# Inverse square roots of a hybrid decoder block: one power on GpSimd in place of a seed and three Newton steps on VectorE

## The chip, the cores and the metric

The kernel runs on one core of a Trainium2 chip. That core has five engines, each with its own instruction queue that runs in order: TensorE (PE in the profile, with its weight loads as PEld), VectorE (DVE), ScalarE (ACT), GpSimd (POOL) and SyncE (SP), which here issues nearly all DMAs. The metric is the device time of one execution in microseconds (us).

## The reference

A decoder layer on 2048 tokens of 1024 channels, float32, with 16 learned meta tokens ahead. What is computed:

```
n1    = rmsnorm(h, norm1_g);  proj = n1 @ w_in              # 1024 x 1024
u, v  = halves of proj
ys    = state space on u (32 groups of 16 channels, 64 complex states), GELU, gate
yp    = trailing means over 2, 4, 8, 16 tokens of v, minus v, times a matrix per group
mixed = concat(rmsnorm(ys, ssm_norm_g), rmsnorm(yp, pool_norm_g));  h = h + mixed @ w_out
n2    = rmsnorm(h, norm2_g)
h     = h + (silu(n2 @ w_gate) * (n2 @ w_up)) @ w_down      # 2816 wide
out   = rmsnorm(h, final_norm_g) without the meta tokens
rmsnorm(x, g) = x * rsqrt(mean(x * x) + 1e-6) * g
```

There are five such norms. Each needs, for every token, one inverse square root of a mean of squares.

## The kernel before

**Tiling.** The tokens form 16 slices of 128 rows (two halves b = 0, 1 of eight slices t each); a seventeenth slice holds the 16 meta tokens. Every float32 product is done as three products of split operands: an operand is cut into a rounded part and a remainder (`split`), ScalarE writing the rounded part and VectorE the remainder, and `mm3` (L123 to L125) multiplies three of the four pairs.

**Stages.** First the input projection of slices 1, 2, meta, 3 to 8, while VectorE and GpSimd work out the tables of the state space (`params`, then eight `units`). Then the state space of b = 0 (`ssm_unit`) together with the projection of slices 9 to 16. Then the output projection: for each of 16 slices `out_mm` multiplies the pooled half and the state-space half of the mixed tokens by `w_out`; in its first eight turns `ssm_unit` of b = 1 runs along. Then the feed-forward network, whose products are formed as seven products of half-size blocks instead of eight (gate and up in `seven`, the down projection in `dmm` and `take`).

**Where inverse square roots are taken.** `rsqrt_into` is called 51 times:

- `stats`, 17 times, one column: the norm of a slice of input tokens. Its result `rs` scales the projected slice when ScalarE moves it out of PSUM (`put_u` L221, `put_v` L228).
- `out_mm`, 16 times, two columns: the norms of both halves of the mixed tokens. TensorE sums the squares into PSUM (`pss`, L814), VectorE scales them into `rv`, and the result `rsp` is used by four operations `hx` on VectorE that add the products to the residual and so free PSUM banks.
- once at the end of each half b, eight columns: the norm ahead of the feed-forward network (`rs2`).
- `finish`, 16 times, one column: the final norm, used by the two operations that scale the output row.

Before the change one call is the scaling `rv` (one operation, two in `out_mm`), then eleven VectorE operations on a tile of 128 x 1, 2 or 8 numbers: a shift (`rsh`, L91), the seed (L93), and three times a square (`rt`, L87), a product (`rt`, L96) and an update (L96). `tt` (L87), `ts` (L91, L93) and `stt` (L96) are helpers, so many operations of the kernel share these lines and are told apart by their tiles.

**What sets the order.** The program is written in the order above, but a planner reorders it when it is built: it places every instruction on its engine's queue by dependencies, priorities and its own estimate of times. Small operations of one call thus stand between larger ones of other calls. At run time each queue is strictly in order, and an instruction waits for semaphores of other engines. The tiles `rv`, `rsh` and `rt` come from a pool with four buffers.

Of the kernel before, what the change touches and what calls it, by code (L numbers as in the profile page):

```python
# [9 lines left out]
F32 = mybir.dt.float32  # L10
# [14 lines left out]
T = 8  # L25
# [14 lines left out]
def kernel(  # L40
# [57 lines left out]
    def rsqrt_into(y, ss, shape, terms):  # L98
        """y = 1 / sqrt(ss * scale + eps); terms: (slice, scale, eps)."""
        n = ss.shape[0]  # L100
        v = small.tile([P] + shape, F32, name="rv", tag="rv")[:n]
        sh = small.tile([P] + shape, I32, name="rsh", tag="rsh")[:n]
        t = small.tile([P] + shape, F32, name="rt", tag="rt")[:n]
        for sl, scale, eps in terms:
            ts(v[sl], ss[sl], scale, M_, eps, A_)
        ts(sh, v.bitcast(I32), 1, ALU.logical_shift_right)
        ts(y.bitcast(I32), sh, -1, M_, 0x5F3759DF, A_)
        for _ in range(3):
            tt(t, y, y, M_)
            stt(t, t, -0.5, v, M_, M_)  # L110
            stt(y, t, 1.5, y, A_, M_)

    def split(hi, lo, src, scale=None, e=V):
        """hi + lo = src (* scale per partition)."""
        if scale is None:
            A.copy(hi, src)  # L116
            tt(lo, src, hi.bitcast(F32), S_, e)
        else:
            A.activation(hi, src, AF.Copy, scale=scale)
            stt(lo, src, scale, hi.bitcast(F32), M_, S_)  # L120
# [5 lines left out]

# [1 line left out]
    ident = const.tile([P, P], F32, name="ident")  # L128
    make_identity(nc, ident)
    ones = const.tile([P, 1], F32, name="ones")  # L130
    V.memset(ones, 1.0)
    ss2 = const.tile([P, 2, NB * T], F32, name="ss2")
    rs2 = const.tile([P, NB * T], F32, name="rs2")
# [22 lines left out]
    def yview(b):  # L156
        """Outputs of the state space, [c, 128 channels, t, channel]."""
        return xu[b].rearrange("c g t h -> c (g t h)").rearrange("c (k t e) -> c k t e", k=4, t=T)

# [1 line left out]
    slices = [(meta, 2 * T)] + [(xv[b][:, t, :], P) for b in range(NB) for t in range(T)]  # L161
# [36 lines left out]
    def load_w(w, cols, spare=(), order=range(KD), then=lambda: None):  # L198
        """Two resident parts of a [D, D] weight, rows scaled."""
        hs, ls = [None] * KD, [None] * KD  # L200
        for n, k in enumerate(order):
            if n < len(spare):
                raw = spare[n]
            else:
                raw = raw_p.tile([P, D], F32, name="wraw", tag="hx")
            SY.dma_start(raw, w[k * P:(k + 1) * P, :])
            if n == 0:
                then()
            hi = wb_p.tile([P, D], F32R, name=f"wh{k}", tag=f"wh{k}")
            lo = wb_p.tile([P, D], F32R, name=f"wl{k}", tag=f"wl{k}")  # L210
            split(hi, lo, raw, cols(k))
            hs[k], ls[k] = hi, lo
        return hs, ls
# [90 lines left out]

# [1 line left out]
    par = ExitStack()  # L306
# [20 lines left out]
    def params():  # L327
# [43 lines left out]
        def exp_into(y, xx):  # L371
            """y = exp(xx), xx is overwritten."""
            k = pa_([P, G], "ek")
            ki = pa_([P, G], "eki", I32)
            ts(xx, xx, -87.0, ALU.max, 88.0, ALU.min)
            ts(k, xx, 1.4426950408889634, M_, MAGIC, A_)
            ts(k, k, -MAGIC, A_)
            stt(xx, k, -0.693359375, xx, M_, A_)
            stt(xx, k, 2.12194440054690583e-4, xx, M_, A_)
            cs = [1.0 / math.factorial(i) for i in range(1, 9)]  # L380
            ts(y, xx, cs[7], M_)
            for c in (cs[6], cs[5], cs[4], cs[3], cs[2], cs[1], cs[0]):
                stt(y, y, c, xx, A_, M_)
            ts(y, y, 1.0, A_)
            ts(k, k, 8388608.0, M_, 127.0 * 8388608.0, A_)
            V.tensor_copy(ki, k)
            tt(y, y, ki.bitcast(F32), M_)
# [121 lines left out]
    def grow(ct, st, w1, w2, n, ck, sk, e1, e2):  # L509
        """Table entries n .. 2n - 1 from 0 .. n - 1 and entry n."""  # L510
        lo, hi = slice(0, n), slice(n, 2 * n)
# [71 lines left out]

    # first two slices side by side: the weights arrive as they are used
    banks = [mm_tile(f"pj{q}") for q in range(4)]
# [59 lines left out]

# [1 line left out]
    ssm = ExitStack()  # L647
    ss_p = ssm.enter_context(tc.tile_pool(name="ssm", bufs=1))

    def rotate(o, tmp, vv, cc, sg, sign, eng=V):  # L650
        """o = vv * (cos + sign * i sin), halves real and imaginary."""
        tt(o, vv, cc, M_)
# [98 lines left out]

# [1 line left out]
    wo = ExitStack()  # L753
# [8 lines left out]
    def out_pool(b, t):  # L762
        """The pooled half of a slice of mixed tokens, by channel."""
        pin = wo_p.tile([P, 4, NCH], F32, name="pin", tag="pin")
# [11 lines left out]
    def out_ssm(b, t, mh, ml, sq):  # L776
        """The half of the state space, and the squares of both."""
        pt = tr_tile("pg")
# [76 lines left out]

# [1 line left out]
    gu = ExitStack()  # L857
# [12 lines left out]
    def turn(b, t):  # L870
        """A normalised row block, by channel, in place."""
        r = norm_row(b, t)
# [16 lines left out]
    def combos(b11, b12, b21, b22, put):  # L889
        """The seven right operands of a two by two product, in place."""  # L890
        put("b11", b11)
# [11 lines left out]
    def x_rows(b, t, direct=()):  # L903
        """The operands of the slice pair (t, t + 4): some are used at once."""
        ra, rb = turn(b, t), turn(b, t + HALF)
# [9 lines left out]
    def w_rows(m):  # L915
        """The sums of the weights of the down projection, rows of tiles 2 m and 2 m + 1."""
        ra, rb = [xa_p.tile([P, D], F32, name="wr", tag="raw", bufs=4) for _ in range(2)]
# [6 lines left out]
    def x_stage(b, i, n):  # L924
        """Operands i .. i + n - 1 from their rows."""
        for nm in XN[i:i + n]:
# [35 lines left out]
    def wset(w, f0):  # L962
        """Parts of a pair of weight tiles for the seven products."""
        r0, r1 = load_raw(w, f0), load_raw(w, f0 + 1)
# [8 lines left out]
    def seven(ws, c, done, early=False):  # L973
        """c(i, j) = weight tile i of the pair times token half j, one product a step."""
        a11, a12, s2, s3, s1, a22, s4 = ws
# [36 lines left out]
    def gate_up(b, f0, wg=None, wu=None):  # L1012
        """Without wu the products with the gate's weights come first, with it they alternate."""
        gt = wc_p.tile([P, 2, 2, 512], F32, name="gt", tag="gt", bufs=3)
# [41 lines left out]

# [1 line left out]
    NM = NF // 2  # L1058
# [90 lines left out]
    def take(i, n, o):  # L1149
        """Adds product i of slice pair n to the blocks that it belongs to."""  # L1150
        b, t = pairs[n]
# [114 lines left out]
```

## Time and profile before

| | |
|---|---|
| time, median of 3 runs | 1911.99 us (1908.38 to 1915.63) |
| profiled execution, span from first to last instruction | 1911.4 us; the page gives no other time of it, and the median of the runs is 0.6 us longer |
| PE busy | 1831.1 us (96%) |
| DVE busy | 1355.2 us (71%), 2553 instructions |
| ACT busy | 677.4 us (35%) |
| POOL busy | 781.4 us (41%), 568 instructions |
| DMA | 298.41 MB, mean 156 GB/s |

How to read it. A stage is a stretch of the span, counted in us from its first instruction. A row of a view by stages gives the stretch, its length, and for each engine its busy time and the number of instructions in it, then the granted TensorE clock (1.00 is full), the share of time the DMA engines were busy and their rate. A row of waits reads "who waited, at which line <- engine, tile and line it waited for: us in total, times, longest". A row of a timeline gives start, duration, engine, line, operation, output <- inputs and shapes; a bracket at its end is the idle time before it and what ended it. Matmuls overlap: 128 x 512 matmuls start 0.23 us apart and last 0.39 us each, so a busy share near 100% can hide small gaps.

### The profile page before, as it was taken

What the parts mean: (1) busy time and instruction counts of PE and PEld (TensorE: products, weight loads), DVE (VectorE), ACT (ScalarE), POOL (GpSimd) and SP (SyncE); (2) the same over time, 40 slices, a digit from 0 to 9 for tenths busy, and PEclk for the clock granted to TensorE, in tenths of its full rate; (3) what the DMA queues carried; (4) which work ended last, traced back from release to release, by engine and by line L of the source; (5) the groups of instructions that cost most, each with busy time, mean ns of one, the idle gap of its engine ahead of it and who ended that gap; (6) DMA issues with size and microseconds to landing.
All of it is one profiled execution on the core that took longest, in us unless ns stands there. A gap on an engine that the chain in (4) does not pass through costs nothing.

```text
span 1911.4 us, 24270 instructions
## 1 busy us (share of the span) xinstructions
PE 1831.1 (96%) x8497; PEld 1502.8 (79%) x8497; DVE 1355.2 (71%) x2553; ACT 677.4 (35%) x1228; POOL 781.4 (41%) x568
## 2 busy tenths in 40 slices
PE   7998996899998999999999999999999999999998
PEld 6776785778887788888887788888888888888876
DVE  6996988998687866666668876666676344445876
ACT  4232334333355332333325333333323343333331
POOL 1583314632143564554546876666562000003300
PEclk9998998899999999999999999999999999999999
DMA  5254425433354443444435663455447765536762
GB/s 179 80 162 159 138 95 171 151 131 121 128 179 152 143 154 94 154 150 137 155 96 183 206 214 127 149 171 176 138 140 234 210 201 178 152 105 209 243 190 90
DMA packets 260524, 298.41 MB, mean 156 GB/s; under 512 B 17149, under 2 KB 204049, under 8 KB 255537
## 3 DMA queue, kind: packets, MB, share of 16 engines
q1 hardware_dynamic: 260304, 296.84, 48.6%
q8 instruction: 67, 1.10, 0.2%
q14 instruction: 57, 0.46, 0.1%
q0 software_dynamic: 96, 0.01, 0.0%
HBM read 202.37 MB, written 96.53 MB: 156 GB/s over the span
## 4 chain that ended last, share of the span: by engine, by line
PE 54%; DVE 18%; issue 15%; DMA 7%; ACT 2%; POOL 2%; SPq 0%; DVEq 0%; POOLq 0%; ACTq 0%
PE pr L125 13%; PE pr L124 13%; PE pr L123 13%; PE pd L124 2%; PE pd L123 2%; PE pd L125 2%; DMA hd<-h_d 2%; DVE z L693 1%; DMA c<-c_d 1%; DVE st L87 1%; DVE wcl L87 1%; PE po L123 1%; PE po L124 1%; PE po L125 1%; DVE rt L87 1%
## 5 line engine op out<-in xcount | busy, mean ns | idle before, releaser
L87 DVE TENSOR_TENSOR wcl<-raw,wch 128x512 fp32r<-128x512 f32 x176 | 178.0, 1014 | 37.6 <-ACT wch L116 36.8
L87 DVE TENSOR_TENSOR fl<-fr,fh 128x512 fp32r<-128x512 f32 x168 | 116.1, 700 | 121.6 <-ACT fh L116 121.5
L116 ACT CAST wch<-raw 128x512 fp32r<-128x512 f32 x176 | 108.5, 620 | 263.2 <-PE pr L124 238.2
L116 ACT CAST fh<-fr 128x512 fp32r<-128x512 f32 x168 | 95.5, 583 | 190.5 <-PE pd L124 165.4
L116 ACT CAST wch<-s 128x512 fp32r<-128x512 f32 x132 | 81.9, 621 | 224.0 <-PE pr L124 177.1
L87 POOL TENSOR_TENSOR s<-raw 128x512 f32<-128x512 f32 x44 | 68.8, 1563 | 183.3 <-DVE wcl L87 85.3
L87 DVE TENSOR_TENSOR wcl<-s,wch 128x512 fp32r<-128x512 f32 x132 | 117.2, 888 | 19.9 <-ACT wch L116 19.8
L87 POOL TENSOR_TENSOR db22h<-db22h,hd 128x512 f32<-128x512 f32 x4 | 5.2, 1295 | 257.0 <-DVE db22h L87 257.0
L123 PE MATMUL po<-wh,mh 128*128 128x512 f32 x256 | 103.5, 404 | 3.1 <-DVE hx L96 2.4
L123 PE MATMUL pj<-wh,xh 128*128 128x512 f32 x256 | 100.6, 402 | 2.5 <-ACT xh L116 2.3
L124 PE MATMUL pj<-wl,xh 128*128 128x512 f32 x256 | 102.9, 403 | 0.0
L125 PE MATMUL pj<-wh,xl 128*128 128x512 f32 x256 | 101.8, 402 | 0.0
L124 PE MATMUL po<-wl,mh 128*128 128x512 f32 x256 | 100.7, 393 | 0.0
L125 PE MATMUL po<-wh,ml 128*128 128x512 f32 x256 | 100.4, 393 | 0.0
L87 POOL TENSOR_TENSOR wr<-wr 128x512 f32<-128x512 f32 x44 | 67.3, 1529 | 70.2 <-DMA wr<-in_w_down_dram 65.9
L87 POOL TENSOR_TENSOR tmp<-z,pk 64x512 f32<-64x512 f32 x32 | 50.8, 1588 | 110.1 <-issue 109.2
L87 DVE TENSOR_TENSOR gt<-gt,ut 128x512 f32<-128x512 f32 x88 | 93.9, 1068 | 0.0
L87 DVE TENSOR_TENSOR gt<-pr,gt 128x512 f32<-128x512 f32 x66 | 45.4, 690 | 58.6 <-PE pr L125 58.5
L87 POOL TENSOR_TENSOR ut<-gt 128x512 f32<-128x512 f32 x22 | 33.1, 1503 | 106.3 <-DVE gt L87 106.3
L1017 ACT ACTIVATE gt<-gt 128x512 f32<-128x512 f32 x88 | 55.5, 632 | 53.9 <-DVE gt L87 53.8
L123 PE MATMUL pr<-xt2h,wch 128*128 128x512 f32 x176 | 69.0, 392 | 4.7 <-DVE gt L87 3.7
L87 POOL TENSOR_TENSOR raw<-raw 128x512 f32<-128x512 f32 x44 | 71.6, 1626 | 0.0
(399 smaller groups left out, 5679.4 us busy)
## 6 DMA issues: line engine op xcount, KB each, us to landing
fr<-ff_d SPq DMA_DIRECT2D x56, 704.0 KB, 5.2
raw<-in_w_gate_dram SPq DMA_DIRECT2D x44, 512.0 KB, 4.7
raw<-in_w_up_dram SPq DMA_DIRECT2D x44, 512.0 KB, 4.2
ff_d<-gt SPq DMA_DIRECT2D x22, 1024.0 KB, 3.9
pk<-pk_d SPq DMA_DIRECT2D x16, 1284.0 KB, 6.1
ff_d<-ut SPq DMA_DIRECT2D x22, 768.0 KB, 5.6
wr<-in_w_down_dram SPq DMA_DIRECT2D x22, 512.0 KB, 3.2
wd_d<-wr SPq DMA_DIRECT2D x22, 512.0 KB, 3.4
```

Source lines behind the costliest of these rows:

```text
L87: e.tensor_tensor(o, a, b, op=op)
L116: A.copy(hi, src)
L123: PE.matmul(o, lh, rh, start=first, stop=False)
L124: PE.matmul(o, lh, rl, start=False, stop=False)
L125: PE.matmul(o, ll, rh, start=False, stop=last)
L693: V.tensor_tensor_scan(z[:, i, 1:], r8[:, g0 + i:g0 + i + 1].to_broadcast([P, NCH]), wr[:, i], z[:, i, 0:1], op0=M_, op1=A_)
L1017: lambda i, j: A.activation(gt[:, i, j], gt[:, i, j], AF.Silu), b == 0 and f0 == 0)
```

## The change

`rsqrt_into` keeps the scaling of the sums into `rv` on VectorE. The eleven operations after it are replaced by one: GpSimd raises `rv` to the power given by a constant tile `mhalf`, filled with -0.5 by one memset at the start. Its result is the same `rs`, `rsp` or `rs2` tile. The tiles `rsh` and `rt` go. Docstrings and comments are dropped too, which moves line numbers: L87 to L96 stay, what is after the constants is two lines earlier (`mm3` four).

```diff
     def rsqrt_into(y, ss, shape, terms):
...
         n = ss.shape[0]
         v = small.tile([P] + shape, F32, name="rv", tag="rv")[:n]
-        sh = small.tile([P] + shape, I32, name="rsh", tag="rsh")[:n]
-        t = small.tile([P] + shape, F32, name="rt", tag="rt")[:n]
         for sl, scale, eps in terms:
             ts(v[sl], ss[sl], scale, M_, eps, A_)
-        ts(sh, v.bitcast(I32), 1, ALU.logical_shift_right)
-        ts(y.bitcast(I32), sh, -1, M_, 0x5F3759DF, A_)
-        for _ in range(3):
-            tt(t, y, y, M_)
-            stt(t, t, -0.5, v, M_, M_)
-            stt(y, t, 1.5, y, A_, M_)
+        m = 1
+        for k in shape:
+            m *= k
+        tt(y, v, mhalf[:n, :m], ALU.pow, GP)
...
     V.memset(ones, 1.0)
+    mhalf = const.tile([P, 2 * T], F32, name="mhalf")
+    V.memset(mhalf, -0.5)
```

The planner then places everything anew. From the first slices of the input projection to the end of the output projection the queues differ, and again in the last two of the seven products of the down projection; GpSimd's queue between the two is the same.

**A turn of the output projection, on VectorE.** `pss` holds the sums of squares, `z` and `st` are the state space's scan and its rotated states, `hx` is the residual row. Before, in one of the turns of b = 0:

```order
L87 TENSOR_TENSOR st<-z,pk 128x512
L93 TENSOR_SCALAR rv<-pss 128x1 x2
L91 TENSOR_SCALAR rsh<-rv 128x2
L93 TENSOR_SCALAR rsp<-rsh 128x2
L87 TENSOR_TENSOR rt<-rsp 128x2
L96 SCALAR_TENSOR_TENSOR rt<-rt,rv 128x2
L96 SCALAR_TENSOR_TENSOR rsp<-rt,rsp 128x2
L87 TENSOR_TENSOR rt<-rsp 128x2
L87 TENSOR_TENSOR st<-st,tmp_4111 128x512
L685 COPY z<-carry 128x4
```

and in two following turns of the changed kernel:

```order
L93 TENSOR_SCALAR rv<-pss 128x1 x2
L87 TENSOR_TENSOR st<-z,pk 128x512
L87 TENSOR_TENSOR st<-st,tmp_3374 128x512
L683 COPY z<-carry 128x4
L96 SCALAR_TENSOR_TENSOR hx<-po,rsp,hx 128x512 x4
...
L87 TENSOR_TENSOR ml<-gt,mh 128x512
L93 TENSOR_SCALAR rv<-pss 128x1 x2
L96 SCALAR_TENSOR_TENSOR hx<-po,rsp,hx 128x512 x3
```

The chain of small operations, which went on behind the copy of `carry` until `hx`, is gone. Between `rv` and the `hx` that needs the power there are three operations in one turn and none in the next.

**The same stage on GpSimd.** `tmp` is half of a rotation of the state space, `sq` and `sqs` sum the squares of the mixed tokens. Before:

```order
L87 TENSOR_TENSOR tmp_4111<-z,pk 64x512 x2
L87 TENSOR_TENSOR sq<-sq 128x2x256
L87 TENSOR_TENSOR sqs<-sq 128x256
L87 TENSOR_TENSOR sq<-sq 128x2x256
L87 TENSOR_TENSOR sqs<-sq 128x256
```

and in the changed kernel:

```order
L87 TENSOR_TENSOR tmp_3698<-z,pk 64x512 x2
L87 TENSOR_TENSOR rsp<-rv,mhalf 128x2
L87 TENSOR_TENSOR tmp_3861<-z,pk 64x512 x2
L87 TENSOR_TENSOR sq<-sq 128x2x256
L87 TENSOR_TENSOR rsp<-rv,mhalf 128x2
L87 TENSOR_TENSOR sqs<-sq 128x256
```

The power stands behind the pair of `tmp` in one turn, and behind a pair and a sum of squares in the next.

**The end of the program, on VectorE.** `ssf` is the sum of squares of an output row, `dt4l` and `db22l` are its two halves. Before:

```order
L87 TENSOR_TENSOR dt4l<-pd,dt4l 128x512
L87 TENSOR_TENSOR ssf<-ss_126 128x1
L93 TENSOR_SCALAR rv<-ssf 128x1
L91 TENSOR_SCALAR rsh<-rv 128x1
L93 TENSOR_SCALAR rs<-rsh 128x1
L87 TENSOR_TENSOR rt<-rs 128x1
L96 SCALAR_TENSOR_TENSOR rt<-rt,rv 128x1
L96 SCALAR_TENSOR_TENSOR rs<-rt,rs 128x1
```

and in the changed kernel:

```order
L87 TENSOR_TENSOR dt4l<-pd,dt4l 128x512
L87 TENSOR_TENSOR ssf<-ss_128 128x1
L93 TENSOR_SCALAR rv<-ssf 128x1
L96 SCALAR_TENSOR_TENSOR dt4l<-dt4l,rs,gf_bc 128x512
L96 SCALAR_TENSOR_TENSOR db22l<-db22l,rs,gf_bc 128x512
```

The scaling of the last rows follows `rv` directly; the power between them is on GpSimd, whose queue holds nothing else by then.

## The prediction

> **What bounds the kernel now.** First the page's busy times, then the view by stages.
>
> ```profile
> PE 1831.1 (96%) x8497; PEld 1502.8 (79%) x8497; DVE 1355.2 (71%) x2553; ACT 677.4 (35%) x1228; POOL 781.4 (41%) x568
> ...
> 60.00:140.00 80.00, 74.43 (x413) 59.49 (x413) 79.69 (x233) 26.81 (x50) 63.90 (x62) 0.98 0.43 130
> 140.00:310.00 170.00, 151.41 (x831) 129.47 (x829) 136.81 (x374) 54.60 (x92) 51.76 (x41) 0.96 0.40 132
> 310.00:420.00 110.00, 91.30 (x490) 80.34 (x491) 100.14 (x177) 39.23 (x88) 56.44 (x40) 0.88 0.46 159
> 420.00:612.00 192.00, 182.54 (x982) 153.64 (x981) 149.20 (x335) 84.15 (x194) 60.92 (x48) 1.00 0.42 140
> 612.00:1780.00 1168.00, 1160.20 (x5045) 942.08 (x5044) 745.15 (x946) 408.12 (x689) 524.33 (x348) 1.00 0.51 162
> 1780.00:1911.40 131.40, 121.95 (x529) 98.78 (x527) 102.78 (x305) 37.93 (x79) 15.01 (x10) 0.98 0.54 176
> ```
>
> After the stretch and its length come PE, PEld, DVE, ACT and POOL. TensorE is the bound as a whole, but not evenly. From 612 to 1780 us it is busy 1160.2 of 1168: nothing that VectorE is spared there can shorten the program. Before 612 it idles 5.6 us of 80, 18.6 of 170, 18.7 of 110 and 9.5 of 192, 52.3 us together, and there VectorE is nearly full: 79.69 of 80 and 100.14 of 110. So the question is how much of these 52.3 us ends because VectorE was late. That is read from TensorE's waits, for the same four stretches in turn:
>
> ```profile
> PE pp L566 <- POOL ptp L87: 4.9, 2, 3.5
> ...
> PE py L703 <- DVE st L87: 6.1, 4, 3.0
> PE pv L679 <- issue: 5.8, 1, 5.8
> PE pvs L688 <- DVE sm L680: 1.8, 1, 1.8
> ...
> PE put L671 <- DVE xl L87: 1.4, 1, 1.4
> ...
> PE py L703 <- DVE st L87: 6.8, 3, 2.7
> PE pss L814 <- POOL sqs L87: 3.8, 1, 3.8
> PE py L702 <- DVE tmp L87: 2.1, 1, 2.1
> PE pvs L688 <- DVE xu L96: 2.0, 1, 2.0
> ...
> PE ppool L771 <- DVE hx L96: 1.0, 1, 1.0
> ...
> PE po L123 <- DVE hx L96: 2.4, 1, 2.4
> PE py L703 <- DVE st L87: 1.9, 2, 1.1
> PE ppool L771 <- DVE hx L96: 1.3, 2, 1.0
> ```
>
> By stretch, late VectorE work ends 4.9 (through GpSimd's `ptp`, which competes with VectorE), 6.1 + 1.8 + 1.4 = 9.3, then 6.8 + 2.1 + 2.0 + 1.0 = 11.9, then 2.4 + 1.9 + 1.3 = 5.6 us: **31.7 us in all**. The 5.8 us behind "issue" are the first load of the state space's tables, which waits for their stores; they stay, and so do waits for ScalarE and for DMAs.
>
> **What goes.** The eleven operations of a call write `rt`, `rsh`, or read them. The view by stages for `rt` alone (nine of eleven), then for `rsh` alone (the other two), same four stretches:
>
> ```profile
> 60.00:140.00 80.00, 14.03 (x43) 0.98 0.43 130
> 140.00:310.00 170.00, 14.04 (x81) 0.96 0.40 132
> 310.00:420.00 110.00, 13.46 (x36) 0.88 0.46 159
> 420.00:612.00 192.00, 28.30 (x122) 1.00 0.42 140
> ...
> 60.00:140.00 80.00, 1.14 (x8) 0.98 0.43 130
> 140.00:310.00 170.00, 2.71 (x18) 0.96 0.40 132
> 310.00:420.00 110.00, 6.49 (x8) 0.88 0.46 159
> 420.00:612.00 192.00, 10.22 (x28) 1.00 0.42 140
> ```
>
> That is 15.2, 16.8, 20.0 and 38.5 us of VectorE's time, 90.4 us before 612, or 19, 12, 20 and 26% of what it is busy with there. It is not 90.4 us of relief. The groups by shape show why:
>
> ```profile
> L91 DVE TENSOR_SCALAR rsh<-rv 128x2 int32<-128x2 int32 x16 | 8.2, 510 | 0.3
> L91 DVE TENSOR_SCALAR rsh<-rv 128x1 int32<-128x1 int32 x32 | 4.8, 150 | 0.7
> ```
>
> The same shift takes 150 ns on one column and 510 ns on two: the two-column calls run where GpSimd is at work. A good part of their time is waiting, which may fall on the next VectorE operation instead. The Trainium skill, page "SBUF — State Buffer", section "SBUF: two separate sides", has a rule for this: GpSimd and a VectorE operation that needs the shared port pair exclude each other for a whole instruction. The rows of 510 and 150 ns agree with it. It also speaks against the change, since each power holds that pair.
>
> **What comes.** One operation per call on GpSimd, and a way there and back. The trace shows no power. The nearest row is an addition on a tile of that size:
>
> ```profile
> L87 POOL TENSOR_TENSOR sum<-sum 128x4 f32<-128x4 f32 x2 | 0.4, 209 | 0.0
> L87 POOL TENSOR_TENSOR sq<-sq 128x512 f32<-128x512 f32 x16 | 22.5, 1409 | 93.8 <-ACT sq L792 85.6 <-ACT sq L773 8.0
> ```
>
> From below, a power costs no less than this addition: 0.2 us. From above, if GpSimd needs as many passes as VectorE did, 11 x 0.209 = 2.3 us. I take 0.5 us, nearer the addition, because it is one instruction of the same size and form. A hop between the engines I take as 0.1 us each, an estimate: over twice the 0.04 us that lies between dependent operations in the last rows below (1904.49 to 1904.53).
>
> A turn of the output projection shows both sides (timelines of GpSimd and of VectorE):
>
> ```profile
> 406.12 3.12 POOL L87 TENSOR_TENSOR tmp<-z,pk 64x512 f32<-64x512 f32 x2 [1.45 <-issue]
> ...
> 406.63 0.22 DVE L93 TENSOR_SCALAR rv<-pss 128x1 f32<-128x1 f32 x2
> ...
> 410.39 0.69 DVE L87 TENSOR_TENSOR st<-st,tmp 128x512 f32<-128x512 f32 x1
> ...
> 411.77 1.41 DVE L96 SCALAR_TENSOR_TENSOR hx<-po,rsp,hx 128x512 f32<-128x512 f32 x2
> ```
>
> Now it is 5.14 us from `rv` to `hx`. In the new order the power stands behind both `tmp`, which end at 409.24, and would end at 409.74, known to VectorE at 409.84; `st` could start at 409.34 and end at 410.03. So `hx` starts near 410.0, 1.8 us sooner, and `st` 1.0 us sooner. With a power of 2.3 us `hx` would start at 411.64: nothing gained.
>
> **The sum before 612.** The waits of 31.7 us are single ones of 0.5 to 3.5 us. A turn that brings `st` and `hx` 1.0 and 1.8 us sooner ends some of them and shortens the longer ones; the copies, scans and evacuations ahead of them stay, and the power puts a little back. I take half in every stretch: 2.5 + 4.7 + 5.9 + 2.8 = **15.9 us**. The ends are 0 and 31.7. The rest of the relief ends in VectorE's idle time, since TensorE then is the bound. Should VectorE have been late for a reason other than load, the relief is worth nothing there.
>
> **After 612.** Sixteen calls of `finish` lie beside the last two products. TensorE is busy 121.95 of 131.4 us there, and most of the rest is the end, after its last matmul. The powers stand behind additions of GpSimd that wait for DMAs, but those also bounded the rows before. I cost this at nothing, covered by TensorE; if VectorE's remainders for the next product came late, each turn would lose the round trip. The last call has no cover:
>
> ```profile
> 1904.34 0.15 DVE L93 TENSOR_SCALAR rv<-ssf 128x1 f32<-128x1 f32 x1
> 1904.53 0.15 DVE L91 TENSOR_SCALAR rsh<-rv 128x1 int32<-128x1 int32 x1
> ...
> 1906.65 0.75 DVE L96 SCALAR_TENSOR_TENSOR dt4l<-dt4l,rs,gf_bc 128x512 f32<-128x512 f32 x1
> ```
>
> From the end of `rv` at 1904.49 to the scaling it is 2.16 us, and will be 0.1 + 0.5 + 0.1 = 0.7: **1.5 us** gained (1.8 with a power of 0.2, a loss of 0.3 with 2.3). The output's store follows as before.
>
> Together 1911.4 - 15.9 - 1.5 = 1894.0 us of span. The median of the runs lies 0.6 us above the profiled span: **1895 us**, 0.9% less. About 0.5%, 9.6 us, is what a measurement of this kernel can tell from no change.
>
> **Rivals.**
>
> *Only the end gains.* TensorE's waits before 612 are not shortened, because VectorE's chains, not its load, set them, or because the new places in the queues cost what the relief gives: `hx` now stands behind a second engine's queue. For it: in the stretch of 420 to 612 TensorE is busy 182.54 of 192 although VectorE has 43 us of idle time, and the new order moves hundreds of TensorE's rows. Against it: 79.69 of 80. Time: 1911.4 - 1.5 + 0.6 = 1910.5 us.
>
> *All waits on VectorE go.* The relief of 90.4 us is nearly three times the 31.7 us of waits. Time: 1911.4 - 31.7 - 1.5 + 0.6 = 1879 us. Against it: the single waits are as long as what one turn gains, or longer.
>
> *The power comes late, and VectorE stands still: slower.* Its place is the output projection, where in some turns `hx` follows `rv` directly, and the power stands behind a sum of squares (1.4 us by its row). VectorE then waits 0.2 us of hops, 1.4 us and the power; what it is spared per turn is (13.46 + 6.49 + 28.30 + 10.22) / 16 = 3.65 us. It decides from a power of 3.65 - 1.6 = 2.05 us on. That GpSimd can be that late shows in the first stage, where a copy of four columns takes twenty times as long as the addition above:
>
> ```profile
> 112.48 4.42 POOL L577 COPY tb<-cA 128x4 f32<-128x4 f32 x1
> ```
>
> At 4 us each of 16 turns loses 1.95 us, 31 us, and the end 2 us: 1911.4 + 31 + 2 + 0.6 = 1945 us. Against it: the copy was late in a stretch where VectorE never rests; in the turns GpSimd's own queue has pauses (1.45 us ahead of `tmp`). By the rule of exclusion named above (the Trainium skill, same page), such lateness grows with VectorE's load, and VectorE's load is what the change lowers.
>
> **How the numbers follow.** The forecast has a chance of 0.50 (its own range 1882 to 1904), only the end 0.28, all waits 0.08, the late power 0.14. The range of 1877 to 1920 holds the first three nearly whole and leaves out the late power and the far end of all waits, some 0.15. Faster by over 0.5% (under 1902.4): 0.46 of the forecast, 0.08, and 0.02 of only the end, 0.56. Within 0.5%: 0.04 and 0.24, 0.28. Slower: 0.14 and 0.02, 0.16.
>
> **What would show it.** In the changed profile: 561 VectorE operations fewer; a power group on GpSimd with a mean near 0.5 us (right up to about 2 us); VectorE's busy time before 612 lower by 50 to 90 us; TensorE's waits for `st`, `tmp`, `xu` and `hx` half as long; the first products of the feed-forward network about 16 us sooner; 1168 us or so from there to the last two products, unchanged; 0.7 us from `rv` to the last `dt4l`. Wrong would be a power of over 2 us, a new wait of VectorE for `rsp` or `rs` of a microsecond a turn, or an unchanged start of the feed-forward network with VectorE idle instead.

## The result and the profile after

The changed kernel takes **1896.8 us** (median of 4 runs, 1896.61 to 1897.31) against 1912.94 us before (4 runs, 1908.38 to 1915.63): a ratio of 0.992, with a 95% interval of 0.9908 to 0.9933. It is 0.7 to 0.9% faster. The forecast was 1895 us.

First the busy times of the changed kernel, from its page:

```profile
PE 1827.5 (96%) x8497; PEld 1499.8 (79%) x8497; DVE 1250.3 (66%) x1993; ACT 681.9 (36%) x1228; POOL 814.5 (43%) x619
```

VectorE has 560 instructions fewer (561 gone, one memset more) and GpSimd 51 more. TensorE, which is the bound, is busy 3.7 us less although it does the same 8497 matmuls, and the span is 16.2 us shorter, so 12.5 us of its idle time went.

Fixed stretches of the span no longer hold the same work, since all of it moved forward. So the two kernels are cut here at the same points of the program: the start of the last product of the input projection (`pj`), of the first of the feed-forward network (`pr`), of the first of the down projection (`pd`), and the last result of TensorE. These rows give two of the points, before and then after (the last two numbers ahead of the semicolon are the first and the last start):

```profile
L125 PE MATMUL pj<-wh,xl x256: 387/389/775, 12.1 to 299.9; 128*128 128x512 f32 x128
L123 PE MATMUL pr<-xb11h,wch x176: 392/398/499, 602.9 to 1457.8; 128*128 128x512 f32 x176
```

```profile
L121 PE MATMUL pj<-wh,xl x256: 387/389/775, 12.1 to 295.5; 128*128 128x512 f32 x128
L119 PE MATMUL pr<-xb11h,wch x176: 392/396/500, 588.0 to 1444.2; 128*128 128x512 f32 x176
```

The view by stages with these cuts, before and then after (stretch, length, then PE, PEld, DVE, ACT and POOL):

```profile
0.00:299.90 299.90, 270.00 (x1430) 223.68 (x1431) 250.91 (x785) 102.62 (x175) 123.46 (x122) 0.97 0.42 134
299.90:602.90 303.00, 269.87 (x1461) 231.34 (x1460) 247.43 (x505) 121.15 (x275) 113.40 (x86) 0.95 0.44 149
602.90:1475.10 872.20, 864.40 (x3760) 700.67 (x3761) 609.79 (x760) 305.54 (x511) 503.40 (x334) 1.00 0.48 156
1475.10:1902.60 427.50, 426.85 (x1849) 347.06 (x1847) 242.93 (x491) 147.37 (x268) 41.12 (x28) 1.00 0.59 180
1902.60:1911.40 8.80, 0.00 (x0) 0.00 (x0) 4.16 (x16) 0.72 (x2) 0.00 (x0) 0.77 0.16 61
```

```profile
0.00:295.50 295.50, 269.44 (x1431) 222.80 (x1431) 228.02 (x599) 104.02 (x175) 133.75 (x139) 0.97 0.43 136
295.50:588.00 292.50, 266.19 (x1461) 229.12 (x1459) 193.62 (x318) 122.36 (x275) 125.40 (x103) 0.95 0.47 154
588.00:1461.50 873.50, 865.55 (x3760) 701.04 (x3761) 608.86 (x749) 304.94 (x509) 505.88 (x335) 1.00 0.49 156
1461.50:1887.80 426.30, 426.27 (x1849) 346.82 (x1847) 217.43 (x326) 149.86 (x269) 48.96 (x43) 1.00 0.59 180
1887.80:1895.20 7.40, 0.00 (x0) 0.00 (x0) 2.42 (x5) 0.72 (x2) 0.55 (x1) 0.72 0.19 71
```

Input part 4.4 us shorter, output projection 10.5, feed-forward 1.3 longer, down projection 1.2 shorter, the end 1.4: together 16.2 us. Ahead of the feed-forward network VectorE is busy 421.6 us in place of 498.3, which is 76.7 less. In the output projection it now rests a third of the time, and TensorE idles 26.3 us there instead of 33.1. TensorE is still not full.

The powers are these groups of GpSimd (by shape; at the end of a row the idle time before them):

```profile
L87 POOL TENSOR_TENSOR rs<-rv,mhalf 128x1 f32<-128x1 f32 x32 | 36.4, 1138 | 134.4 <-DVE rv L93 131.4 <-DVE sm L87 1.9 <-DVE sm L678 1.0
L87 POOL TENSOR_TENSOR rsp<-rv,mhalf 128x2 f32<-128x2 f32 x16 | 13.7, 857 | 40.1 <-DVE rv L93 39.9
L87 POOL TENSOR_TENSOR rs<-rv,mhalf 128x8 f32<-128x8 f32 x2 | 3.7, 1834 | 0.8 <-DVE rv L93 0.8
```

The means hide how much single ones differ. By tile, most powers are near the shortest of each group:

```profile
L87 POOL TENSOR_TENSOR rs<-rv,mhalf x35: 539/551/9123, 11.7 to 1889.8; 128x1 f32<-128x1 f32 x32, 128x8 f32<-128x8 f32 x2, 16x1 f32<-16x1 f32 x1
L87 POOL TENSOR_TENSOR rsp<-rv,mhalf x16: 699/707/1212, 334.7 to 582.0; 128x2 f32<-128x2 f32 x16
```

A power takes 0.55 us on one column and 0.70 us on two (minimum, median, maximum in ns). But one of them took 9.1 us, and two others in the first stage 5.97 and 3.41. How such a one looks is seen in the timelines of VectorE and of GpSimd:

```profile
127.14 0.13 DVE L93 TENSOR_SCALAR rv<-ss 128x1 f32<-128x1 f32 x1
127.20 0.34 DVE L87 TENSOR_TENSOR tb<-tb,tw 128x64 f32<-128x64 f32 x2
...
132.17 0.74 DVE L87 TENSOR_TENSOR n<-n,n9t 128x576 f32<-128x576 f32 x1
134.56 0.23 DVE L87 TENSOR_TENSOR tb<-tb,cA 128x64 f32<-128x64 f32 x1 [1.65 <-POOL tb L573]
```

```profile
127.35 5.97 POOL L87 TENSOR_TENSOR rs<-rv,mhalf 128x1 f32<-128x1 f32 x1 [3.03 <-DVE rv L93]
133.29 1.05 POOL L87 TENSOR_TENSOR ptp<-xr,y 128x512 f32<-128x512 f32 x1
134.29 0.24 POOL L573 COPY tb<-eb 128x64 f32<-128x64 f32 x1
```

VectorE runs two-input additions and products without a pause from 127.20 to 132.91. The power starts at 127.35 and ends only at 133.32, 0.4 us after the last of them. Behind it stand `ptp`, and the copy that VectorE itself wants next, so VectorE then stops for 1.65 us. This power was held up beside a row of eighteen VectorE instructions. The Trainium skill, page "SBUF — State Buffer", section "SBUF: two separate sides", has the port pair shared by the two engines locked for a whole instruction. The trace bears that out in part only. At the place above GpSimd did not get in between the instructions of a row either; but beside other unbroken rows of the same kind of work a power passed almost unhindered, and VectorE did not slow down (timelines of GpSimd and VectorE, merged):

```profile
144.71 0.60 POOL L87 TENSOR_TENSOR rs<-rv,mhalf 128x1 f32<-128x1 f32 x1 [3.98 <-DVE rv L93]
144.82 0.27 DVE L87 TENSOR_TENSOR tb<-tb,cA 128x128 f32<-128x128 f32 x1
```

Five VectorE operations of 0.20 to 0.28 us run during those 0.60 us, in a row without a pause from 134.56 to 148.26. What decides whether a power is held up is left open.

TensorE's waits in the changed kernel, for 60 to 140, 140 to 310 and 310 to 420 us in turn; from 420 to 612 none longer than 0.2 us on VectorE or GpSimd is left:

```profile
PE pp L564 <- POOL ptp L87: 6.6, 2, 5.2
...
PE py L701 <- DVE st L87: 6.2, 3, 3.0
...
PE pvs L686 <- DVE sm L678: 2.5, 1, 2.5
...
PE pv L677 <- issue: 0.4, 1, 0.4
...
PE py L701 <- DVE st L87: 5.9, 3, 2.5
...
PE py L700 <- DVE tmp L87: 2.1, 1, 2.1
...
PE po L119 <- DVE hx L96: 0.8, 1, 0.8
```

And VectorE has a new wait, seen in its waits over the whole span and in one turn of the output projection (timelines of GpSimd and VectorE, merged):

```profile
DVE hx L96 <- POOL rsp L87: 13.6, 12, 2.0
DVE rv L93 <- PE pss L812: 8.7, 2, 4.7
```

```profile
415.34 0.21 DVE L93 TENSOR_SCALAR rv<-pss 128x1 f32<-128x1 f32 x2
415.37 1.29 POOL L87 TENSOR_TENSOR sq<-sq 128x512 f32<-128x512 f32 x1 [1.88 <-ACT sq L790]
416.62 0.70 POOL L87 TENSOR_TENSOR rsp<-rv,mhalf 128x2 f32<-128x2 f32 x1
...
417.36 1.41 DVE L96 SCALAR_TENSOR_TENSOR hx<-po,rsp,hx 128x512 f32<-128x512 f32 x2 [1.80 <-POOL rsp L87]
```

The power stands behind a sum of squares, and VectorE stands still for 1.80 us. Even so `hx` starts 2.0 us after `rv`, where the Newton steps took 5.1.

The end, in the timeline of all engines:

```profile
1889.54 0.15 DVE L93 TENSOR_SCALAR rv<-ssf 128x1 f32<-128x1 f32 x1
1889.84 0.55 POOL L87 TENSOR_TENSOR rs<-rv,mhalf 128x1 f32<-128x1 f32 x1 [7.00 <-DVE rv L93]
1890.42 0.75 DVE L96 SCALAR_TENSOR_TENSOR dt4l<-dt4l,rs,gf_bc 128x512 f32<-128x512 f32 x1 [0.73 <-POOL rs L87]
```

From the end of `rv` (1889.69) it is 0.15 us to the power, 0.55 us of power, 0.03 us to the scaling: 0.73 us, where it was 2.16.

### The profile page after: what moved, and what is told of

It reads as the page before. It is cut to its first block, busy times and chain, and to the rows that moved or that the text cites. A ratio compares the mean times of both kernels' runs of the same rounds, so it can differ in the third digit from the quotient of the medians.

```text
span 1895.2 us, 23776 instructions
## 1 busy us (share of the span) xinstructions
PE 1827.5 (96%) x8497; PEld 1499.8 (79%) x8497; DVE 1250.3 (66%) x1993; ACT 681.9 (36%) x1228; POOL 814.5 (43%) x619
## 4 chain that ended last, share of the span: by engine, by line
PE 73%; DVE 2%; DMA 2%; POOL 1%; ACT 1%; issue 1%; DVEq 0%; POOLq 0%; ACTq 0%
PE pr L119 14%; PE pr L120 14%; PE pr L121 14%; PE pd L119 8%; PE pd L120 7%; PE pd L121 7%; PE po L119 2%; PE po L121 2%; PE po L120 2%; DMA xp<-xr_d 1%; PE ptx L874 1%; PE pgate L783 1%; DMA hr<-h_d 1%; DVE wcl L87 1%; PE ppool L769 0%
## 5 line engine op out<-in xcount | busy, mean ns | idle before, releaser
L87 DVE TENSOR_TENSOR wcl<-raw,wch 128x512 fp32r<-128x512 f32 x176 | 178.0, 1014 | 37.7 <-ACT wch L112 36.7
L87 DVE TENSOR_TENSOR fl<-fr,fh 128x512 fp32r<-128x512 f32 x168 | 116.0, 702 | 127.5 <-ACT fh L112 120.7
L87 POOL TENSOR_TENSOR s<-raw 128x512 f32<-128x512 f32 x44 | 67.7, 1540 | 173.3 <-DVE wcl L87 72.3
L87 DVE TENSOR_TENSOR wcl<-s,wch 128x512 fp32r<-128x512 f32 x132 | 117.6, 892 | 20.5 <-ACT wch L112 20.2
L87 POOL TENSOR_TENSOR db22h<-db22h,hd 128x512 f32<-128x512 f32 x4 | 5.2, 1291 | 256.4 <-DVE db22h L87 256.4
L87 POOL TENSOR_TENSOR rs<-rv,mhalf 128x1 f32<-128x1 f32 (+2 forms) x35 | 40.6, 1160 | 154.9 <-DVE rv L93 151.8
L87 POOL TENSOR_TENSOR wr<-wr 128x512 f32<-128x512 f32 x44 | 67.3, 1530 | 72.9 <-DMA wr<-in_w_down_dram 67.8
L87 DVE TENSOR_TENSOR gt<-gt,ut 128x512 f32<-128x512 f32 x88 | 94.0, 1069 | 0.0
L87 POOL TENSOR_TENSOR tmp<-z,pk 64x512 f32<-64x512 f32 x32 | 49.7, 1553 | 84.3 <-issue 82.4
L87 DVE TENSOR_TENSOR gt<-pr,gt 128x512 f32<-128x512 f32 x66 | 45.4, 690 | 58.6 <-PE pr L121 58.4
L87 POOL TENSOR_TENSOR ut<-gt 128x512 f32<-128x512 f32 x22 | 33.4, 1520 | 107.7 <-DVE gt L87 107.7
```

The lines of the kernel that those rows point to most:

```text
L87: e.tensor_tensor(o, a, b, op=op)
```

## The experiments

Three theories were set against each other. **LOAD**: VectorE has less to do, so all that it owes TensorE comes sooner. **CHAIN**: the way from a sum of squares to its root is shorter, and the load does not matter. **ORDER**: the planner, given other instructions, found another order of the queues that happens to be better. A fourth, **PLACE** against **PRICE**, came up on the way. All times are medians; the last three columns come from one profiled execution each (start of the last `pj`; from there to the first `pr`; from the last start of `pd` to the end of the span). The first two of these columns are good to 3 or 4 us only: out_only and out_pow3 run the same operations in the same order on TensorE, VectorE, ScalarE and GpSimd through the whole input part, and differ by 3.9 us there; changed, stats_only, rv_act_out and early_root do so too, and lie between 292.2 and 295.6. Every kernel but before has been placed anew by the planner, so each comparison holds what another order of the queues does, and only where the order is said to be the same is that excluded.

| kernel | time, us | ratio to before | input part | output part | end |
|---|---|---|---|---|---|
| before | 1911 to 1913 | 1 | 299.9 | 303.0 | 9.3 |
| changed | 1896.8 | 0.9908 to 0.9933 | 295.5 | 292.5 | 7.8 |
| out_only | 1902.8 | 0.9928 to 0.9964 | 300.3 | 294.0 | 9.3 |
| stats_only | 1907.6 | 0.9962 to 0.9984 | 294.9 | 303.1 | 9.3 |
| pow_load | 1908.0 | 0.9967 to 0.9985 | 300.1 | 301.5 | 7.8 |
| add_v | 1880.8 | 0.9823 to 0.9857 | 290.9 | 283.0 | 7.5 |
| add_gp | 1888.1 | 0.9862 to 0.9889 | 293.3 | 289.1 | 7.4 |
| out_pow3 | 1907.6 | 0.9971 to 0.9994 | 296.4 | 298.6 | 9.3 |
| rv_act | 1890.9 | 0.9867 to 0.9900 | 293.3 | 291.2 | 7.7 |
| rv_act_out | 1897.5 | 0.9917 to 0.9942 | 295.6 | 295.4 | 7.8 |
| rv_act_stats | 1896.3 | 0.9915 to 0.9940 | 292.7 | 297.2 | 7.8 |
| early_root | 1908.4 | 0.9972 to 0.9995 | 292.2 | 303.3 | 7.8 |
| best | 1909.2 | 0.9978 to 1.0005 | 295.7 | 305.3 | 7.8 |
| early_newton | 1921.2 | 1.0045 to 1.0070 | 299.4 | 313.9 | 9.3 |

**One part of the change at a time.** `rsqrt_into` gets a switch, and the calls that are not under test keep the eleven operations:

```
+        if power:
             tt(y, v, mhalf[:n, :m], ALU.pow, GP)
+        else:
+            (shift, seed and three Newton steps on VectorE, as before)
 out_only:    power=False in stats, rs2 and finish
 stats_only:  power=False in out_mm, rs2 and finish
```

> Only the sixteen calls of the output projection take their inverse roots from GpSimd; the statistics of the input rows, rs2 and the last norms keep the Newton steps on VectorE. Between the first product of the output projection and the first of the feed-forward network the changed kernel is 10.5 us shorter (286.1 to 275.6 us). Theory LOAD (VectorE is spared 3.65 us a turn, and TensorE's waits there shrink) and theory CHAIN (the way from rv to hx is shorter): both expect that part of the gain alone, about 1902 us against 1912.9 before, with the rest of the program as before. Theory ORDER (the planner's other order of the queues happened to be the better one, the operations matter little): no such share, anything between 1900 and 1913 us, and stretches before the output projection that change too.

> Only the seventeen calls of stats take the power on GpSimd; the output projection, rs2 and the last norms keep Newton. In the changed kernel the first product with a state space table starts 0.9 us sooner and the last input projection 4.4 us sooner than before. LOAD: about 1912.9 - 4.4 = 1908.5 us. CHAIN: the roots of the input rows are wanted long after they are ready, so nothing is gained: 1912 to 1914 us. ORDER: no link to these shares. In all of them the powers beside the building of the tables (60 to 140 us) should again be stretched to 3 to 9 us each, if a VectorE that never rests is what stretches them.

Both came out as LOAD (and, for out_only, CHAIN) had it: 1902.8 and 1907.6 us, 9.6 and 4.8 us under the 1912.4 us of the kernel before in that series. The table shows each gain where its calls are: 9.0 us in the output part of out_only, 5.0 us in the input part of stats_only, and nothing elsewhere. With 1.5 us at the end the two gains of the medians make 15.9 of the 16.1 us; that they fit so closely is in part luck, since each has an interval of 4 us or more. CHAIN, which expected nothing from stats, falls for that part. The powers beside the tables were stretched in stats_only as well, two of them to 3.41 and 5.97 us as in the changed kernel; the one of 9.1 us took 0.60 us there.

**The relief taken back.** The power stays, and VectorE does the eleven operations as well, into a tile `ry` that nothing reads:

```
         tt(y, v, mhalf[:n, :m], ALU.pow, GP)
+        (shift, seed and three Newton steps of v into ry, on VectorE)
```

> The changed kernel, and VectorE still does the eleven operations of every call, into a tile that nothing reads: the power's shorter chain stays, the relief of VectorE is taken back. LOAD: most of the gain before the last products goes, about 1909 to 1914 us; what stays is at most the end. CHAIN: hx still follows the power, so most of the gain stays, 1897 to 1901 us. ORDER: the planner makes a third order, with no forecast.

1908.0 us, 4.5 us under the 1912.4 us before. Of the 16.1 us some 11.6 are gone; 1.5 of what stays is the end, which no longer waits for VectorE's steps. The input part is back at 300.1 us and the output part at 301.5. So most of the gain goes with VectorE's load. The two theories do not come apart cleanly, since the idle steps stand in the queue that leads to `hx` too: from the end of `rv` to the first `hx` of a turn it is 4.6 us before, 1.8 us in the changed kernel and 3.4 us here (medians of sixteen turns; `rv` itself moves in the queue as well). Not quite half of the shortening stays, and 1.5 of the 10.5 us of the output part. The chain, as far as it is kept, leaves 3 us in all, a little more than LOAD expected and far from the 12 us of CHAIN; that is net of what the power costs on GpSimd, which this kernel still pays.

**One addition on VectorE, or on GpSimd.** How much more would the relief bring if GpSimd were not asked? The mean square is scaled to almost nothing and one addition of a typical inverse root stands for the power, once on each engine:

```
-            ts(v[sl], ss[sl], scale, M_, eps, A_)
+            ts(v[sl], ss[sl], scale * 1e-6, M_, eps, A_)
-        tt(y, v, mhalf[:n, :m], ALU.pow, GP)
+        tt(y, v, mhalf[:n, at:at + m], A_)         # add_v
+        tt(y, v, mhalf[:n, at:at + m], A_, GP)     # add_gp
```

> In place of the power stands one addition on VectorE (the mean square times 1e-6 plus a typical inverse root, so the norms are only roughly right: this part of the computation is changed). VectorE is spared ten of eleven operations, and GpSimd has no part in it. LOAD alone, with the powers on GpSimd costing nothing elsewhere: as the changed kernel less 0.7 us at the end, 1896 us. If the stretched powers beside the tables (9.1, 6.0 and 3.4 us, with a stop of VectorE of 1.65 us behind one of them) hold the tables up: 1889 to 1893 us, with the first product with a state space table 3 to 6 us sooner. If GpSimd's place behind VectorE is what gives the gain (VectorE goes on to other work meanwhile), slower than the changed kernel: 1899 to 1905 us.

> The addition of add_v (the mean square times 1e-6 plus a typical inverse root, so the norms are only roughly right: this part of the computation is changed), but on GpSimd, where the changed kernel has the power: same place, same hops, a cheaper operation. add_v took 1880.8 us, the changed kernel 1896.8: 16 us between an operation on VectorE and a power on GpSimd. Theory PRICE (the power itself is long, 0.55 us on one column and 0.70 on two): most of the 16 us goes, 1882 to 1887 us, and the output projection (first product of it to first of the feed-forward network, 275.3 us in the changed kernel, 267.6 in add_v) takes 268 to 270 us. Theory PLACE (VectorE stands in its own queue behind another engine's, and GpSimd starves beside a VectorE that never rests, whatever it computes): 1892 to 1897 us, 273 to 276 us for the output projection, 10 to 13 us of VectorE waits for rsp, and additions stretched to 3 us and more beside the tables.

add_v took 1880.8 us, 8 us less than any of its expectations: GpSimd costs the changed kernel 16 us, as much as it gains. My forecast of 1896 us for "the powers on GpSimd cost nothing elsewhere" was wrong by that much. add_gp lies in the middle at 1888.1 us, between what PRICE (to 1887) and PLACE (from 1892) had said, so neither holds alone: 8.7 us are the power's price against an addition, 7.3 us the place. The first figure is the cleaner one: the changed kernel and add_gp have nearly the same queues (GpSimd's differ in two operations of 619, VectorE's in some 26 of 1993). Those of add_v are others, so the 7.3 us hold what the order does as well. The views of add_gp show both. Its groups of additions, by shape:

```profile
L87 POOL TENSOR_TENSOR rs<-rv,mhalf 128x1 f32<-128x1 f32 x32 | 16.9, 528 | 140.9 <-DVE rv L93 132.4 <-DVE step L93 5.4 <-DVE sm L87 1.9
L87 POOL TENSOR_TENSOR rsp<-rv,mhalf 128x2 f32<-128x2 f32 x16 | 4.3, 266 | 37.4 <-DVE rv L93 37.3
```

its VectorE waits:

```profile
DVE rv L93 <- PE pss L813: 20.9, 5, 5.3
DVE hx L96 <- POOL rsp L87: 11.9, 13, 1.8
```

and two of its additions beside the tables (timeline of GpSimd):

```profile
88.74 3.06 POOL L87 TENSOR_TENSOR rs<-rv,mhalf 128x1 f32<-128x1 f32 x1 [1.23 <-DVE rv L93]
...
125.76 5.61 POOL L87 TENSOR_TENSOR rs<-rv,mhalf 128x1 f32<-128x1 f32 x1 [3.04 <-DVE rv L93]
```

An addition of 0.19 to 0.37 us elsewhere beside the tables takes 5.61 us where the power took 5.97, behind the same idle time. So these stretches are not the power's own. VectorE waits almost as long for `rsp` (11.9 us against 13.6) with an operation of a third of the length: most of that wait is the queue ahead of it. The longest power of all (9.1 us, near 57 us) has no like in add_gp or stats_only, and its cause is left open: stats_only has the same queues there, and the power took 0.60 us beside the same row of VectorE.

**Where does the power become too long?** In out_only every power of the output projection is done three times:

```
+            for _ in range(3):
                 tt(y, v, mhalf[:n, :m], ALU.pow, GP)
```

> out_only, with every power of the output projection done three times over: with 0.70 us each, 1.4 us more at least between rv and hx, 2.1 us in all. The prediction put the point from which the change loses at a power of 2.05 us. If VectorE stands still for all of it (16 turns of 1.4 us): up to 22 us above out_only, 1925 us. If the prediction's break-even holds: 1910 to 1915 us, and VectorE's waits for rsp go from 12.6 us to 25 to 35. If VectorE has other work to do meanwhile: 1903 to 1907 us.

1907.6 us, 4.8 us more than out_only by the medians (some 7 by the ratios), so still faster than before. VectorE's waits doubled, as the break-even of the prediction would have it:

```profile
DVE hx L96 <- POOL rsp L87: 26.7, 13, 3.3
```

But 14.1 us more of them lengthened the program by 5 to 7 us only, a third to a half of them, less than the break-even had it (1910 to 1915 us) and a little more than "VectorE has other work meanwhile" (to 1907). The rest, as I read it, fell where TensorE had work. GpSimd spent 40.5 us on these powers in place of 13.7, 1.67 us more a turn, and a fifth to a quarter of that reaches the end. By that rate the 9.6 us of out_only would be used up at a power of 3 to 4 us, not at 2.05 us. That is a rough estimate: the two intervals allow a difference of 1 to 13 us, and the queues of the output part are not the same.

**Attempts at a better place.** The scaling `rv` on ScalarE, so that VectorE has no part ahead of the power; for stats and the output projection, and for either alone:

```
+            if act:
+                A.activation(v[sl], ss[sl], AF.Copy, bias=eps, scale=scale)
+            else:
                 ts(v[sl], ss[sl], scale, M_, eps, A_)
```

> The changed kernel, and the scaling ahead of the power (rv) goes to ScalarE for stats and the output projection: VectorE has no part before the power. Theory LOAD: VectorE is spared 49 operations more (some 10 us) and its 8.7 us of waiting for the sums of squares; the output projection takes about 270 us in place of 275.3, the total 1888 to 1893 us. Theory PLACE: ScalarE's queue is a third one to stand in, rsp comes later, VectorE's waits for rsp grow beyond 13.6 us and the total is 1896 to 1903 us.

> As rv_act, but only for the output projection; stats scales on VectorE as in the changed kernel. Up to the first product of the output projection (312.7 us) it should be as the changed kernel within 1 us, so that the two parts of rv_act come apart. LOAD: 1890 to 1894 us. PLACE: 1896 to 1902 us.

> The half of rv_act that came out well: the scaling ahead of the power goes to ScalarE for the statistics of the input rows only. rv_act reached the output projection 7.3 us sooner than the changed kernel (305.4 against 312.7 us) and lost 3.8 us in it (279.1 against 275.3). If the two parts add: 1896.8 - 7.3 = 1889.5 us, a little under rv_act's 1890.9. If the planner's new order spoils it, or rv_act's gain was the order's: 1892 to 1897 us. No power beside the tables longer than 2 us.

rv_act is the fastest kernel that computes the whole function: 1890.9 us, as LOAD had it in total, 1.0 to 1.3% under the kernel before, and its interval does not touch that of the changed kernel. But its cause was not settled. In the output projection alone it brought nothing (PLACE: 1897.5 us), and for stats alone it brought 0.5 us where 7 were expected. There the input part came out as in rv_act (292.7 us, against 293.3), no power of rv_act between 60 and 160 us was longer than 1.2 us, and yet the output part, whose code is that of the changed kernel, was 4.7 us longer than there. VectorE's queue there is another one (181 of its 317 operations stand in the order of the changed kernel), so ORDER fits, in a kernel where I had not counted on it; it was not tested by itself. The second thing expected of rv_act_stats failed too: its queues ahead of the output part are those of rv_act, and yet one power, near 58 us, took 5.64 us.

The roots of the output projection a turn early, with the sums of squares and `rv`, as text that moves from `out_mm` to the end of `out_ssm`; with the power (early_root), with the power and ScalarE's `rv` for stats (best), and with Newton steps (early_newton):

```
 def out_ssm(...):
     tt(sqs, sq[:, :, 0], sq[:, :, 1], A_, GP)
+    pss = tr_tile("pss") ... rsp = small.tile(...); rsqrt_into(rsp, pss[:, 0, :2], ...)
-    return mh, ml, sqs
+    return mh, ml, rsp
 def out_mm(b, t, mh, ml, rsp, pooled=None):
-    pss = ... rsqrt_into(rsp, ...)
```

> The changed kernel, and the sums of squares over the channels, rv and the power of a slice of the output projection stand right behind the squares, a turn before the products that need them; nothing else is changed. Theory PLACE: VectorE's 13.6 us of waits for rsp go, and the output projection takes about 268 to 271 us in place of 275.3: 1889 to 1893 us in all. Rival: VectorE then waits as long for the sums of squares (rv behind pss), which are only called for earlier: 1895 to 1899 us.

> rv_act_stats and early_root together. If both act where they should, they add: 7 us ahead of the output projection and 4 to 7 us in it, 1883 to 1886 us, between add_v (1880.8) and add_gp (1888.1). If one of them does nothing: as the other, 1889 to 1893 us.

> The kernel before, with the roots of the output projection computed a turn early as in early_root, still by Newton steps on VectorE. CHAIN: hx no longer stands behind eleven dependent operations, and much of the 9.6 us that the power brought to the output projection comes without it: 1903 to 1907 us. LOAD: VectorE has as much to do as before, nothing is gained: 1910 to 1914 us.

All three missed. VectorE's waits in early_root:

```profile
DVE rv L93 <- PE pss L796: 22.0, 8, 6.1
DVE hx L96 <- POOL rsp L87: 9.2, 9, 2.7
```

The 13.6 us for `rsp` became 9.2, and the 8.7 us for the sums of squares became 22.0: VectorE now stands, earlier in its queue, before what is not ready. This was the rival there, but dearer than it said: 1908.4 us, 11.6 more than the changed kernel, and best is no better. The waits need not be all of it: the mean granted clock of the output part is 0.92 in early_root, against 0.95 in the changed kernel. early_newton is 9.9 us slower than the kernel before. The pair early_newton and early_root is the control that ORDER needed: in quite another order of the queues, the same exchange of Newton steps for a power brings 1921.23 - 1908.36 = 12.9 us, against 16.1. Moving this text costs some 10 us in both kernels, so the order matters as much as many a change; but the gain does not hang on one order. How many of the 16.1 us are the order's own, two orders can't say.

## Why the prediction held, step by step

**The time.** 1895 us was forecast (own range 1882 to 1904) and 1896.8 measured. In its total, the case "half of the waits and the end" is the one that occurred. Faster by over 0.5% had 0.56.

**The sum before 612.** Forecast 15.9 us. The first product of the feed-forward network starts 14.9 us sooner (602.9 to 588.0). The total is right; how it was made up is not, so that it came out so close is luck:

- *By stretch.* 7.2 us were put ahead of 310 us and 8.7 behind. Measured: 4.4 us in the input part, 10.5 in the output projection. In the first stage nothing was gained where I had 2.5: the wait of `pp` for `ptp` even grew from 4.9 to 6.6 us. Powers stretched to 3.4 to 9.1 us stand there, with `ptp` and the table copies behind them, and the one of 5.97 us cost VectorE 1.65 us. How much of the relief they ate in all is not shown: in stats_only the one of 9.1 us took 0.60, and the input part was only 0.6 us shorter. The copy of 4.42 us in the prediction had warned of this; I used it only for the rival.
- *By wait.* The listed waits of 31.7 us are now 6.6 + 8.7 + 8.8 + 0 = 24.1: they lost 7.6 us, not 15.9. The 5.8 us of `pv`, which the prediction said would stay, are 0.4, but little of that is a gain: the load itself is only 0.9 us sooner (`pv` starts at 166.44 instead of 167.34), and TensorE starts its last product ahead of it at 165.7 instead of 161.1 us, with five matmuls fewer done. And TensorE is busy 3.7 us less in the output projection for the same 1461 matmuls. Waits on one engine were too narrow a measure of what late work costs, and half of them happened to be near the whole gain.
- *The waits for `st`, `tmp`, `xu`, `hx`* were to halve: 23.6 us became 15.0.

**The power.** 0.5 us taken, 0.55 and 0.70 measured; hops 0.1 each taken, 0.15 and 0.03 measured. The bounds (0.2 and 2.3) held for undisturbed powers.

**The turn that was worked out.** It is the fourth one; in the changed kernel (timelines of GpSimd and VectorE):

```profile
398.39 3.08 POOL L87 TENSOR_TENSOR tmp<-z,pk 64x512 f32<-64x512 f32 x2 [2.87 <-issue]
...
401.51 0.69 DVE L87 TENSOR_TENSOR st<-st,tmp 128x512 f32<-128x512 f32 x1 [2.53 <-POOL tmp L87]
401.56 1.21 POOL L87 TENSOR_TENSOR rsp<-rv,mhalf 128x2 f32<-128x2 f32 x1
402.80 2.73 DVE L96 SCALAR_TENSOR_TENSOR hx<-po,rsp,hx 128x512 f32<-128x512 f32 x4 [0.51 <-POOL rsp L87]
```

The power stands behind both `tmp`, as forecast. Counted from the start of `tmp`, `st` comes 1.15 us sooner than before (forecast 1.0) and `hx` 1.24 us (forecast 1.8), because the power beside `st` takes 1.21 us and not 0.5. Here the mechanism was right.

**The shift of 510 and 150 ns.** The prediction put the difference down to where the calls run. The trace before says otherwise: one-column shifts beside a GpSimd product or sum (at 108.44, 123.94 and 205.98 us) take 0.14 to 0.15 us, while two-column ones take 1.00 to 1.25 us in six of sixteen calls, each beside GpSimd's `tmp` or its work on the rows `hr`. So where a call runs is not the whole reason. That part of a two-column call is waiting still holds.

**VectorE's load.** 50 to 90 us less before 612 was the mark; 76.7 us it was. pow_load shows that most of the gain goes when this load comes back.

**The end.** Forecast 1.5 us, measured 1.4 (2.16 to 0.73 us between `rv` and the scaling). Costing the other fifteen calls at nothing was right: the two stretches from 602.9 to 1902.6 us are 0.1 us longer together.

**The rival "late power".** Its mechanism is there: a power behind a sum of squares, VectorE idle for 1.8 us, 13.6 us in 12 waits. The prediction named "a new wait of VectorE for `rsp` of a microsecond a turn" as a sign of being wrong. The wait came, 0.85 us a turn, and the time held, so the sign was badly chosen. The failing step is "each turn loses": it took every microsecond of VectorE's standstill as one of the program. By out_pow3 a third to a half of it arrives.

**What it overlooked.** The relief as such was worth nearly twice the forecast. "All waits on VectorE go" was priced at 1879 us with a chance of 0.08 on the ground that single waits are as long as what a turn gains. add_v, with ten of eleven operations gone and no GpSimd, takes 1880.8. The change got half of it not because half of the waits are of another kind, but because GpSimd took the other half back: 8.7 us by the power's length, 7.3 by its place and whatever the order adds to it.

## What to carry to other kernels

Work taken from a full engine pays where the bound engine waits for that engine, even in operations of 0.15 us. But price the place where it goes: on GpSimd a tiny operation costs its own time, the queue ahead of it, and in places a row of VectorE work beside it. When a planner sets the order, make every comparison under a second order as well, since moving text alone was worth 10 us here.

## What the runs showed of the hardware that was not expected

- A row of two-input operations on VectorE can hold up a one-column GpSimd operation over many instructions: 5.97 us for a power and 5.61 us for an addition at the same place, against 0.55 and 0.19 us undisturbed. It does not always: powers at 75.24, 108.52 and 144.71 us took 0.54, 0.73 and 0.60 us beside rows of the same kind, and the one of 3.41 us at 89.54 ended while its row went on to 103.53.
- A power on GpSimd takes some 0.16 us more for every column, an addition does not: the shortest powers are 0.54 us for one column, 0.70 for two and 1.65 for eight, the shortest additions in add_gp 0.19, 0.19 and 0.20 us.
- The same 1461 matmuls of the output projection kept TensorE busy 269.87 us before and 266.19 after. The mean granted clock of that part is 0.95 in both rows above, so what made the difference stays open.
